# A decoder layer's channel stage on two halves of 528 tokens, seven products for each block

## The chip, the cores and the metric

The kernel runs on one core of a Trainium2 chip. The metric is the device time of one execution in microseconds: 1078.13 us is the median of three runs of the kernel before (1078.03 to 1078.82). TensorE (PE) multiplies matrices into PSUM, which has eight banks of 2 KB per partition; VectorE (DVE), ScalarE (ACT) and GpSimd (POOL) work on SBUF and PSUM, each with its own queue of instructions in a fixed order; SyncE (SP) issues most transfers.

## The reference

One decoder layer on 1056 tokens (1024 of a prompt and 8 x 4 decode tokens), with 1024 channels, 2816 hidden channels (22 chunks of 128) and float32 throughout. What the change touches begins at the norm ahead of the feed-forward part:

```
    m, pool_state = _pool_mixer(u, pool_prev, pos0, w_pool, pool_scale)
    mix = jnp.concatenate([a, m], axis=-1) @ w_out
    x = x + _rms(mix, n_mix_post)
    f = _rms(x, n_ffn_pre)
    f = (jax.nn.silu(f @ w_gate) * (f @ w_up)) @ w_down
    x = x + _rms(f, n_ffn_post)
    x = x + jax.nn.sigmoid(x @ w_ple_gate) * (p @ w_ple)
    return x, k_state, v_state, pool_state
```

## The kernel before

Channels lie on partitions and tokens along the free axis. TensorE reads float32 in a rounded form, so each operand is split into a high and a low part (`split`: a cast on ACT at L167, a subtraction on DVE at L168), and each product is three matmuls, high x high, high x low and low x high (`gemm`, L126 for each matmul). Each matmul loads its own 128 x 128 weights.

The tokens form three groups of 352 (`N`), one matmul wide each. From the channel norm on, groups 0 and 1 are taken together in Strassen's way (Winograd's form): a 2 x 2 block product with seven products in place of eight, named P1, P2, P4, S1 to S4, over operands B11, B21, B22 and T1 to T4, which are sums of the blocks of the input; for the gate and up products the two block columns are the two token groups, the block rows are the gate and up rows of one chunk, and the sum runs over two halves of 512 channels. S1 to S4 also need sums of weights, formed on POOL (L1132). Group 2 is computed directly with eight quarter products. `WALK` sets the order: five slabs of two chunks for group 2 alone, which stand beside the norms of groups 0 and 1, then eleven slabs for the other two or for all. The direct down products of group 2 (`down`) are interleaved with them (`downs`).

The hidden activations of groups 0 and 1 are combined to the seven operands (`pair_put`), split, and written to DRAM (`stage`, `spill`); `down7` reloads them (`x_get`) and works the down product in steps of `STEPS`: a product of a few chunk pairs at a time into one or four banks, which are then added into SBUF (L1286). After it come the norm of the result, the residual, and the last stage: sigmoid of a gate product (seven products again for groups 0 and 1, `ple_first` and `ple_rest`; eight for group 2, `ple_out`) times an embedding product (`embed`).

The order of work is the order in which the code issues it, with norms and similar chains of DVE and ACT work kept as generators (`chain`, `step`, `finish`) that are advanced between matmuls as these are issued (`turn`). Weights are loaded and split some items ahead (`need`, `w_load`). PSUM is a pool of eight single banks. Ahead of twelve products a matmul of 64 columns is issued (`spacer`).

Of the kernel before, what the change touches and what calls it, by code (L numbers as in the profile page):

```python
# [10 lines left out]
F32 = mybir.dt.float32  # L11
# [28 lines left out]
AHEAD = 5  # L40
# [11 lines left out]
W_RAW = 3  # L52

# [8 lines left out]
def trunk_kernel(  # L62
# [38 lines left out]
    psum = ctx.enter_context(tc.tile_pool(name="psum", bufs=8, space=bass.MemoryType.PSUM))  # L101
# [27 lines left out]

    def bank():  # L130
        return psum.tile([P, 512], F32, tag="b", name=nm("b"))

    def tmp(n, s="t", dt=F32):
        return spool.tile([P, n], dt, tag="tmp", bufs=5, name=nm(s), padded_shape=[P, NX])

    def kept(s):
        return spool.tile([P, N], F32, tag="hk", bufs=4, name=nm(s))
# [76 lines left out]
    FIRST2 = tuple(range(NSLAB - 2 * AHEAD, NSLAB, 2))  # L214
    WALK = [(s, (2,)) for s in FIRST2]
    WALK += [(s, (0, 1) if s in FIRST2 else (0, 1, 2)) for s in range(NSLAB)]
    LAST2 = len(WALK) - 1
# [9 lines left out]
    WGU, WD = [], []  # L227

    def down_at(n, i):

        if not n or 2 not in WALK[n - 1][1]:
            return ()
        if 2 in WALK[n][1]:
            return () if i else (0, 1)
        return (i,)

    for n, (s, gs) in enumerate(WALK):
        pairs_of = []
        for i in range(SLAB):
            c = SLAB * s + i  # L240
            jg = direct_item(w_gu[c, 0], [P, KC, P])
            if gs != (0, 1, 2):
                ju = direct_item(w_gu[c, 1], [P, KC, P])
            for j in down_at(n, i):
                WD[n - 1].append(direct_item(w_dn[WALK[n - 1][0], j], [P, SLAB, 512]))
            if gs == (0, 1, 2):
                ju = direct_item(w_gu[c, 1], [P, KC, P])
            js = item("sums", ITEMS[jg][1][0], ITEMS[ju][1][0]) if 0 in gs else None
            pairs_of.append((jg, ju, js))
        WGU.append(pairs_of)  # L250
        WD.append([])
    WD[-1] = [direct_item(w_dn[WALK[-1][0], j], [P, SLAB, 512]) for j in range(2)]
# [3 lines left out]
    QUARTER = {"P1": "11", "P2": "12", "P4": "22"}  # L256
    FIVE, TWO = ("P1", "P4", "P2", "S3", "S2"), ("S1", "S4")
    OPERAND = {"P1": "B11", "P2": "B21", "P4": "T4", "S2": "T2", "S3": "T3", "S1": "T1", "S4": "B22"}
    STEPS = [(k, (0, 1)) for k in FIVE + TWO]
    STEPS += [(k, at) for at in ((2, 3), (4, 5)) for k in FIVE]  # L260
    STEPS += [(k, (2, 3, 4, 5)) for k in TWO]
    SUMS_AT = ["P2", "P2"] + ["P4"] * 4
    WDN = {}
    for k, at in STEPS:
        for e in at:
            WDN[k, e] = item("quarter" if k in QUARTER else "dsum", k, e, at if e == at[-1] else ())
    WPE = [[], []]

    def plan_ple(n, m):
        wp = direct_item(w_ple[m // 4], [P, 2, 512]) if m % 4 == 0 else WPE[n][-1][0]  # L270
        WPE[n].append((wp, direct_item(w_pg[m], [P, KC, P])))

    for m in range(KC):
        plan_ple(0, m)


    PAIRS = ((7, 6), (1, 0), (3, 2), (5, 4))
    W1 = {a: WPE[0][a] if a == KC - 1 else None for a, _ in PAIRS}
    wp1 = WPE[0][-1][0]
    wp0 = None  # L280
    for a in (5, 3, 1):
        if a == 3:
            wp0 = item("home", add_plan(w_ple[0], [P, 2, 512]))
        W1[a] = (wp0 if a < 4 else wp1), direct_item(w_pg[a], [P, KC, P])
    RAW2 = {}
    for a, b in PAIRS:
        if a == KC - 1:
            RAW2[a] = tuple(ITEMS[WPE[0][m][1]][1][0] for m in (a, b))
        else:
            ja = ITEMS[W1[a][1]][1][0] if a == 1 else add_plan(w_pg[a], [P, KC, P])  # L290
            RAW2[a] = ja, add_plan(w_pg[b], [P, KC, P])
    HALF = {KC - 1: WPE[0][KC - 2][1]}
    W2 = {}
    for (a, _), (nxt, _) in zip(PAIRS, PAIRS[1:] + PAIRS[:1]):
        if nxt < KC - 1:
            HALF[nxt] = item("half", RAW2[nxt][1])
        W2[a] = HALF[a], item("sums", *RAW2[a])

    in_a.update(ITEMS[W1[a][1]][1][0] for a in (3, 1))
    in_a.update(j for a in (3, 5) for j in RAW2[a])  # L300
# [3 lines left out]
    quarters = {}  # L304

    def q_load(q, e):

        if (q, e) not in quarters:
            n = len(SETS[e])
            shape = [P, n, 512]  # L310
            if q == "11" and e > 1:
                t = wpool.tile(shape, F32, tag="wr", bufs=W_RAW, name=nm("wq"))
            else:
                t = act_tile(shape, s="wq")
            s0 = SETS[e][0]
            row, col = int(q[1]) - 1, int(q[0]) - 1
            nc.sync.dma_start(t, w_dn[s0 : s0 + n, col, :, row, :].rearrange("s p n -> p s n"))
            quarters[q, e] = t
        return quarters[q, e]

    def q_loads(kind, js):
        for q in {"P1": ("11",), "P4": ("22", "21"), "P2": ("12",)}.get(js[0], ()):
            q_load(q, js[1])
# [17 lines left out]
    def need(k, ahead=LOOK):  # L341

        for i in range(len(made), max(k + 1, min(k + ahead + 1, until[0]))):
# [9 lines left out]
            elif kind == "quarter":  # L353
                made[i] = q_split(q_load(QUARTER[js[0]], js[1]))
                if js[0] == SUMS_AT[js[1]]:
                    for n in ("S1", "S3", "S2"):
                        for e in js[2]:
                            q_sum(n, e)
# [1273 lines left out]
```

## Time and profile before

| | |
|---|---|
| median of the runs | 1078.13 us |
| profiled execution, span | 1076.7 us |
| granted clock of TensorE | 0.997 |
| PE busy | 1065.5 us, 6805 matmuls |
| DVE, ACT, POOL busy | 828.7, 525.7, 285.5 us |
| first gate product to last matmul | 264 to 1071 us |
| moved by DMA | 162.01 MB, 150 GB/s |

The span is measured from the first to the last instruction of one profiled execution. In a row of the trace's groups stand line, engine, operation, output <- inputs and shapes, the number of instructions, then the busy time and the mean of one in ns, then the idle time ahead of them and what ended it. In the chain of waits, time and length are followed by the engine and line, or by what the step waited for.

### The profile page before, as it was taken

The page shows a single profiled execution, that of the slowest core. Times are in us where ns is not written, and L with a number is a line of the kernel's source. Part 1 is how long each engine was busy: PE and PEld are TensorE (multiplying, and loading weights), DVE is VectorE, ACT ScalarE, POOL GpSimd, SP SyncE. Part 2 cuts the span into 40 slices and gives each one's busy share as a digit, 9 for nine tenths or more (in the row PEclk, how much of TensorE's full clock was granted, in tenths as well). Part 3 has the DMA queues.
Part 4 walks back from the last instruction along what each step waited for, and adds up shares of the span by engine and source line. Part 5 has one row for each costly group of instructions (what it writes and reads, how often), then busy time and mean ns, then how long its engine had stood idle before and what let it go on. Part 6 is the DMA issues. An engine that isn't in the chain of part 4 may idle for free.

```text
span 1076.7 us, 17467 instructions
## 1 busy us (share of the span) xinstructions
PE 1065.5 (99%) x6805; PEld 1049.6 (97%) x6805; DVE 828.7 (77%) x1229; ACT 525.7 (49%) x951; POOL 285.5 (27%) x213
## 2 busy tenths in 40 slices
PE   9999999999999999999999999999999999999997
PEld 8999988899999999999999999999999999999997
DVE  6766378977979957767758758659668877999898
ACT  8522277776855524344434434434344832476542
POOL 1045022200000032422324223232309076401170
PEclk9999999999999999999999999999999999999999
DMA  8121311352644312352441533614876955836422
GB/s 299 60 72 40 108 54 37 136 217 90 228 154 134 109 40 81 144 186 71 159 168 59 212 114 107 236 43 160 310 267 230 405 189 181 310 114 216 138 67 74
DMA packets 54162, 162.01 MB, mean 150 GB/s; under 512 B 5796, under 2 KB 20164, under 8 KB 54080
## 3 DMA queue, kind: packets, MB, share of 16 engines
q1 hardware_dynamic: 52752, 159.13, 42.2%
q10 hardware_dynamic: 1328, 1.77, 0.5%
q8 instruction: 53, 0.87, 0.4%
q14 instruction: 29, 0.24, 0.1%
HBM read 123.02 MB, written 37.86 MB: 149 GB/s over the span
## 4 chain that ended last, share of the span: by engine, by line
PE 91%; DVE 5%; ACT 2%; issue 1%; DMA 0%; ACTq 0%; SPq 0%; DVEq 0%
PE b L126 90%; DVE sl L168 1%; DVE sg L1439 1%; PE b L120 1%; DVE u L1286 1%; DVE ql L168 1%; DVE yo L1440 1%; DVE p L1476 0%; DMA xr<-in_x_dram 0%; ACT a L780 0%; DVE w L168 0%; DVE acc L930 0%; ACT qh L167 0%; DVE u L1476 0%; ACT sg L1436 0%
## 5 line engine op out<-in xcount | busy, mean ns | idle before, releaser
L126 PE MATMUL b<-fh,wh 128*128 128x352 f32 x720 | 231.4, 322 | 0.0
L126 PE MATMUL b<-fl,wh 128*128 128x352 f32 x716 | 229.3, 320 | 0.0
L126 PE MATMUL b<-fh,wl 128*128 128x352 f32 x716 | 229.2, 320 | 0.0
L1132 POOL TENSOR_TENSOR wr<-wr 128x512 f32<-128x512 f32 x47 | 69.1, 1470 | 538.1 <-DVE wl L168 512.4
L168 DVE TENSOR_TENSOR wl<-wr,wh 128x1024 fp32r<-128x1024 f32 (+1 forms) x123 | 162.9, 1326 | 51.3 <-ACT wh L167 51.2
L167 ACT CAST wh<-wr 128x1024 fp32r<-128x1024 f32 (+1 forms) x123 | 126.1, 1027 | 123.1 <-PE b L126 96.5
L126 PE MATMUL b<-xo,qh 128*128 128x352 f32 x620 | 147.7, 321 | 0.5 <-ACT u L1314 0.5
L126 PEld LDWEIGHTS b<-fh,wh 128*128 128x128 f32 x720 | 134.9, 188 | 0.0
L126 PE MATMUL b<-fh,sh 128*128 128x352 f32 x420 | 134.6, 322 | 0.0
L126 PEld LDWEIGHTS b<-fl,wh 128*128 128x128 f32 x716 | 134.5, 188 | 0.0
L126 PE MATMUL b<-fh,sl 128*128 128x352 f32 x416 | 133.2, 320 | 0.9 <-DVE sl L168 0.9
L126 PEld LDWEIGHTS b<-fh,wl 128*128 128x128 f32 x716 | 134.1, 187 | 0.0
L126 PE MATMUL b<-fl,sh 128*128 128x352 f32 x416 | 133.2, 320 | 0.0
L126 PE MATMUL b<-h,wh 128*128 128x352 f32 x480 | 112.6, 325 | 1.4 <-ACT h L504 1.2
L126 PEld LDWEIGHTS b<-xo,qh 128*128 128x128 f32 x620 | 107.1, 188 | 0.7 <-ACT u L1314 0.7
L126 PE MATMUL b<-xo,ql 128*128 128x352 f32 x308 | 99.1, 322 | 1.4 <-DVE ql L168 1.2
L339 POOL TENSOR_TENSOR wq<-wq,wq 128x512 f32<-128x512 f32 x44 | 77.4, 1797 | 66.0 <-DVE ql L168 56.3
L167 ACT CAST st<-c 128x352 fp32r<-128x352 f32 x55 | 26.8, 487 | 122.8 <-DVE c L1201 96.6
L126 PEld LDWEIGHTS b<-h,wh 128*128 128x128 f32 x480 | 83.3, 190 | 2.5 <-ACT h L504 1.4
L168 DVE TENSOR_TENSOR sl<-wr,sh 128x1024 fp32r<-128x1024 f32 x47 | 59.5, 1266 | 33.1 <-ACT sh L167 33.1
L126 PE MATMUL b<-hid,wh 128*128 128x352 f32 x352 | 84.0, 321 | 0.0
L126 PEld LDWEIGHTS b<-fh,sl 128*128 128x128 f32 x416 | 77.9, 187 | 1.2 <-DVE sl L168 1.2
(211 smaller groups left out, 2177.8 us busy)
## 6 DMA issues: line engine op xcount, KB each, us to landing
wr<-in_w_gu_dram SPq DMA_DIRECT2D x64, 512.0 KB, 3.4
xd<-st SPq DMA_DIRECT2D x35, 704.0 KB, 4.9
xo<-xd SPq DMA_DIRECT2D x35, 704.0 KB, 6.1
wr<-in_w_dn_dram SPq DMA_DIRECT2D x22, 512.0 KB, 4.2
wq<-in_w_dn_dram SPq DMA_DIRECT2D x20, 512.0 KB, 9.6
wr<-in_w_pg_dram SPq DMA_DIRECT2D x10, 512.0 KB, 3.5
x<-in_x_dram SPq DMA_DIRECT2D x6, 704.0 KB, 9.1
x1d<-x SPq DMA_DIRECT2D x6, 704.0 KB, 3.3
```

Source lines behind the costliest of these rows:

```text
L120: ins = te.transpose(out, src, ident)
L126: ins = te.matmul(*args, **kw)
L167: fix(se.copy(hi, src))
L168: fix(ve.tensor_tensor(lo, src, hi.bitcast(F32), op=ALU.subtract))
L339: ge.tensor_tensor(*(q_load(q, e)[:, i, :] for q in (out, a, b)), op=op)
L1132: ge.tensor_tensor(out, a, b, op=op)
L1286: ve.tensor_tensor(out, a, b, op=ALU.add)
L1439: ve.tensor_tensor(sg[:, v], sg[:, v], pp[:, v], op=ALU.mult)
L1440: ve.tensor_tensor(yo[:, v], sg[:, v], xm[:, v], op=ALU.add)
```

## The change

From the channel norm on, the 1056 tokens form two halves of 528, each in two runs of 264 columns (`QN`, `HN`), and all of them take the seven products; no group is computed directly. A tile of 264 columns has rows 320 apart (`PITCH`). PSUM is a pool of four pairs of banks; a product fills one run per bank, and one DVE or ACT instruction evicts both runs.

- The first product P1 and the gate's C11 = P1 + P2 are made ahead of the blocks, for each run by itself and in the order `AHEAD`, because the tokens become ready group after group; the parts are written to DRAM (`p_d`), and read again in `chunk`. The gate weights are loaded for this once more.
- `chunk` makes the other five products for one block.
- `down` takes one product after the other over all 11 chunk pairs, with its four output tiles in all four PSUM pairs. Operands are written unsplit, reloaded for each product and split then. The weight sums are made on POOL with 1024 columns at a time (`down_form`).
- `ple_steps` and `finished` are the norm and residual of a half; the last stage takes pairs of output tiles, all of them with seven products.
- The spacers are removed.

```diff
-AHEAD = 5
+QN = T // 4
+HN = 2 * QN
+PITCH = 320
+
+
+PARTS = {0: ((1, 0, 0, 352),), 1: ((0, 352, 0, 176), (1, 352, 176, 176)), 2: ((0, 0, 0, 352),)}
+FIRST = 14
...
-    psum = ctx.enter_context(tc.tile_pool(name="psum", bufs=8, space=bass.MemoryType.PSUM))
+    psum = ctx.enter_context(tc.tile_pool(name="psum", bufs=4, space=bass.MemoryType.PSUM))
...
+    def pair():
+        return psum.tile([P, 2, 512], F32, tag="b", name=nm("b"))
+
+    spare = []
+
     def bank():
-        return psum.tile([P, 512], F32, tag="b", name=nm("b"))
+        if spare:
+            return spare.pop()
+        t = pair()
+        spare.append(t[:, 1, :])
+        return t[:, 0, :]
...
+    def row(s="r"):
+        return tmp(HN, s).rearrange("p (i n) -> p i n", n=QN)
+
+    def runs(dt=F32, s="f"):
+        return act_tile([P, 4, PITCH], dt, s)[:, :, :QN]
...
+    AHEAD = [(c, (0,)) for c in range(FIRST)]
+    AHEAD += [(c, (0, 1)) for c in range(FIRST, FFC)]
+    AHEAD += [(c, (1,)) for c in range(FIRST)]
...
+        if k == "S2":
+            keeps[e] = r[0]
+            add(r[0], r[0], r[1], ALU.add)
+            add(r[0], r[0], r[2], ALU.subtract)
+        elif k == "S3":
+            add(r[0], r[0], r[1], ALU.subtract)
+        elif k == "S1":
+            add(r[0], keeps[e], r[0], ALU.add)
+        elif k == "S4":
+            add(r[0], r[0], keeps[e], ALU.subtract)
+        hl = w_tile(r[0].shape, "qh"), w_tile(r[0].shape, "ql")
+        split(*hl, r[0])
...
-    def spacer(w, x):
-        mm(bank()[:, :SPACER], w, x[:, :SPACER], start=True, stop=True)
...
+    def product(w, x, onto=None):
+
+        ps = pair()[:, :, :QN] if onto is None else onto
+        for i in range(2):
+            gemm(ps[:, i, :], ops4(w, x, i), onto=onto is not None)
+        return ps
...
+    def ahead(w, c, i):
+
+        wg = need(w)
+        ps = bank()[:, :QN]
+        gemm(ps, ops4(quarter(wg, 0), operand("B11", i), i))
+        st = row("st")
+        se.copy(st[:, 0, :], ps)
+        if second:
+            second.pop()()
+
+        def rest():
+            gemm(ps, ops4(quarter(wg, 1), operand("B21", i), i), onto=True)
+            se.activation(st[:, 1, :], ps, AF.Silu)
+            nc.sync.dma_start(p_d[c][:, :, i, :], st)
+
+        second.append(rest)
...
+    def seven(w, sums, p1, x, last):
+
+        p4 = product(need(w), x("T4"))
+        s = need(sums)
+        add(p1, p1, product(s["S2"], x("T2")))
+        u4 = row("u4")
+        if not last:
+            add(u4, p1, product(s["S4"], x("B22")))
+        u3 = row("u3")
+        add(u3, p1, product(s["S3"], x("T3")))
+        c21 = row("c21")
         add(c21, u3, p4)
-        ve.tensor_tensor(c21, c21, c11, op=ALU.mult)
-        p5 = product(s["S1"], f7["T1"])
+        yield c21
+        p5 = product(s["S1"], x("T1"))
         add(u3, u3, p5)
-        add(p1, p1, p5)
-        add(p1, p1, product(s["S4"], f7["B22"]))
-        se.activation(p1, p1, AF.Silu)
-        ve.tensor_tensor(u3, u3, p1, op=ALU.mult)
-        if late is None:
-            pair_put(pair, slot, c21, u3)
+        yield u3
+        if last:
+            add(p1, p1, p5)
+            yield p1, product(s["S4"], x("B22"))
         else:
-            late.append((pair, slot, c21, u3))
-
-    os_ = [None] * G
-
-    def down(n, m):
-        wh, wl = need(WD[n][m // 4])
+            add(u4, u4, p5)
+            yield u4
...
+    def chunk(c):
+
+        part_load(c + 2)
+        p = parts.pop(c)
+        p1, c11 = p[:, 0], p[:, 1]
+        made7 = seven(*WG[c], p1, operand, False)
+        c21 = next(made7)
+        add(c21, c21, c11, ALU.mult)
+        c22 = next(made7)
+        c12 = next(made7)
+        se.activation(c12, c12, AF.Silu)
+        add(c22, c22, c12, ALU.mult)
+        chunk_put(c, c21, c22)
...
+    def finished(b):
+
+        for h in range(2):
+            sqs = [runs(s="sq") for _ in range(2)]
+            for sq, o in zip(sqs, os_[b][h]):
+                se.activation(sq, o, AF.Square)
+            add(sqs[0], sqs[0], sqs[1])
+            if h == 0:
+                first = sqs[0]
+                yield 8, 0
+        add(first, first, sqs[0])
+        yield 16, 0
+        acc3[b] = tmp(HN, "acc")
+        add(acc3[b].rearrange("p (i n) -> p i n", n=QN), first[:, 0:2, :], first[:, 2:4, :])
+        for m in range(KC):
+            o = os_[b][m // 4][m % 4 // 2][:, 2 * (m % 2) : 2 * (m % 2) + 2, :]
+            se.activation(o, o, AF.Identity, scale=gn[:, 3, m : m + 1])
+        yield 5, 0
...
+    def x_get(n):
+        if n < len(DOWN) * NSLAB:
+            k, c = DOWN[n // NSLAB], n % NSLAB
+            t = runs(F32R, "xo")
+            src = t[:, 2:4, :].bitcast(F32)
+            nc.sync.dma_start(src, spilled[OPERAND[k], c])
+            split(t[:, 0:2, :], t[:, 2:4, :], src)
+            xops[n] = t
+
+    def down(k, banks, onto=False, ends=None, order_=(0, 1, 2, 3)):
+
+        n0 = DOWN.index(k) * NSLAB
+        for e, ps in enumerate(SETS):
+            for i, c in enumerate(ps):
+                x_get(n0 + c + 3)
+                wh, wl = need(WDN[k, e], 2)
+                t = xops.pop(n0 + c)
+                for j in order_:
+                    cols = slice(j * P, (j + 1) * P)
+                    if banks[j] is None:
+                        banks[j] = pair()[:, :, :QN]
+                    for q in range(2):
+                        gemm(
+                            banks[j][:, q, :],
+                            [(wh[:, i, cols], wl[:, i, cols], t[:, q, :], t[:, 2 + q, :])],
+                            c == 0,
+                            c == NSLAB - 1,
+                            onto=onto,
+                        )
+                    if c == NSLAB - 1:
+                        ends(j, banks[j])
...
+    for w, (c, qs) in zip(WA, AHEAD):
+        for i in qs:
+            ahead(w, c, i)
+    second.pop()()
+    part_load(0)
+    part_load(1)
+    for c in range(FFC):
+        chunk(c)
+        if c == FFC - 1:
+            for n in range(3):
+                x_get(n)
+
+    share[0] = 0.5
+    u = out_half()
+    banks = [None] * 4
+    down("P1", banks, ends=lambda j, ps: se.copy(at_j(u, j), ps))
+    os_[0][0] = c11 = out_half()
+    down("P2", banks, onto=True, ends=lambda j, ps: se.copy(at_j(c11, j), ps))
+    down("S2", [None] * 4, ends=lambda j, ps: add(at_j(u, j), at_j(u, j), ps))
+    u3 = out_half()
+    down("S3", [None] * 4, ends=lambda j, ps: add(at_j(u3, j), at_j(u, j), ps))
+    os_[0][1] = c21 = out_half()
+    down("P4", [None] * 4, ends=lambda j, ps: add(at_j(c21, j), at_j(u3, j), ps))
+    chain(ple_steps(0, 1e6), 8)
+    n = len(summed)
+
+    def both(j, ps):
+        v = row("p5")
+        se.copy(v, ps)
+        add(at_j(u, j), at_j(u, j), v)
+        add(at_j(u3, j), at_j(u3, j), v)
+
+    down("S1", [None] * 4, ends=both)
+    while len(summed) == n:
+        step(chains[0])
+    step(chains[0])
+    down("S4", [None] * 4, ends=lambda j, ps: add(at_j(u, j), at_j(u, j), ps))
+    os_[1] = [u, u3]
...
+    finish(list(chains))
     share[0] = 0.7
...
+    chain(ple_steps(1, 12), 4)
+    p1s = {}
+    for a, _ in PAIRS:
+        w = need(W1[a])
+        ps = product(quarter(w, 0), e7["B11"])
+        p1s[a] = row("p1")
+        se.copy(p1s[a], ps)
+        xm = x2_row(a, 0)
+        pp = embed(WE[a // 4], a, 0)
+        product(quarter(w, 1), e7["B21"], ps)
+        ple_end(ps, xm, pp, a, 0)
+    for w, h in ((WE[0], 0), (WE1, 1)):
+        for a, b in PAIRS:
+            if a // 4 == h:
+                for m, half_ in ((b, 0), (b, 1), (a, 1)):
+                    embed_early(w, m, half_)
     for a, b in PAIRS:
...
+        last = (a, b) == PAIRS[-1]
+        xm = {x: x2_row(*x) for x in ((b, 0), (b, 1), (a, 1))}
+        made7 = seven(*W2[a], p1s[a], gate_operand, last)
+        for x in ((b, 0), (b, 1), (a, 1)):
+            v = next(made7)
```

On TensorE, inside the gate and up loop, at a border of two products (the names are the PSUM tile, the high or low part of the operand, and the high or low part of the summed weights). Before:

```order
L126 MATMUL b_6171<-fl_3647,sh_6058 128x352
L126 MATMUL b_6171<-fh_3646,sl_6059 128x352
L126 MATMUL b_6186<-fh_3847,sh_6054 128x352
L126 MATMUL b_6186<-fl_3848,sh_6054 128x352
L126 MATMUL b_6186<-fh_3847,sl_6055 128x352
```

And now:

```order
L133 MATMUL b_6699<-fh_4358,sh_6302 128x264
L133 MATMUL b_6699<-fh_4356,sl_6303 128x264
L133 MATMUL b_6728<-fh_4417,sh_6302 128x264
L133 MATMUL b_6728<-fh_4419,sh_6302 128x264
L133 MATMUL b_6728<-fh_4417,sl_6303 128x264
```

The three matmuls per product and their weights are the same; each has 264 columns, and a product runs through its weights twice, once for each run.

On ACT, where the down stage goes from S1 to S4 (L1339 copies S1's four results out of PSUM; `acc` is the sum of squares, and L427 makes its inverse root from the pair `b_10496`):

```order
L1339 COPY p_10462<-b_10097 128x528
L189 CAST xo_10506<-xo_10506 128x2x264
L1339 COPY p_10472<-b_10104 128x528
L1339 COPY p_10482<-b_10118 128x528
L189 CAST xo_10553<-xo_10553 128x2x264
L1339 COPY p_10492<-b_10125 128x528
L427 ACT_TABLE_LOAD
L427 ACTIVATE acc_10254<-b_10496,c_86 128x528
```

Before, the mean had a bank of its own out of eight; now its pair is one of four, and its reader stands behind the four copies.

On ACT, at the head of the last stage. Before (L1423 copies an embedding out of PSUM, L1436 is the sigmoid, L1254 scales the down result):

```order
L167 CAST wh_9993<-wr_9952 128x1024
L1254 ACTIVATE u_8425<-u_8425,c_72 128x352
L1436 ACT_TABLE_LOAD
L1436 ACTIVATE sg_10047<-b_10005 128x352
L167 CAST wh_9999<-wr_9991 128x1024
L1423 COPY pp_10053<-b_10054 128x352
```

And now (L1402 copies a first part P1 out of PSUM, L1386 is the sigmoid, L1216 squares, L1227 scales):

```order
L1402 COPY p_10941<-b_10904 128x528
L189 CAST wh_10892<-wr_10884 128x1024
L1386 ACT_TABLE_LOAD
L1386 ACTIVATE sg_10988<-b_10904 128x528
L189 CAST wh_10898<-wr_10890 128x1024
L189 CAST pl_10911<-pr_10913 128x4x264
L1216 ACTIVATE sq_10936<-o_8278 128x4x264
L1216 ACTIVATE sq_10937<-o_8279 128x4x264
L1216 ACTIVATE sq_10964<-o_9368 128x4x264
L1216 ACTIVATE sq_10965<-o_9369 128x4x264
L1227 ACTIVATE o_8278<-o_8278,c_72 128x2x264 x2
L1227 ACTIVATE o_8279<-o_8279,c_72 128x2x264 x2
```

Two more such rows of L1227 (o_9368, o_9369) follow, and behind them stands the next copy, of `b_10999`, onto which TensorE goes on adding. Before, the scaling at the border was the last of several that stood among the down products, one tile of 352 columns at a time; now squares and scalings of a whole half stand as one block in the last stage.

More of the change, by code (lines that the diff above doesn't have):

```diff
@@ L321, in q_loads @@
[L321 to L339 removed]
+    keeps = {}
@@ new lines, in plans, with down_form, add @@
+    def plans(kind, js):
+        return DN_LOADS[js] if kind == "down" else js
+    def down_form(k, e):
+        r = [raws[j] for j in DN_LOADS[k, e]]
+        def add(out, a, b, op):
+            ge.tensor_tensor(out, a, b, op=op)
+        if k == "S2":
+            keeps[e] = r[0]
[9 more added lines that the diff above has]
+        split(*hl, r[0])
+        return hl
@@ L381, in trunk_kernel, with step @@
     share = [0.6]
+    def step(ch):
+        try:
+            load, wait = next(ch[0])
+        except StopIteration:
+            chains.remove(ch)
+            return
+        dve[0] = max(dve[0], now[0]) + load / share[0]
+        ch[1] = dve[0] + wait
     def turn(n):
@@ new lines, in ffn_steps @@
+            yield 18, 0
+        if g:
+            i = 2 - g
+            for h in range(2):
+                key = f"B{h + 1}1"
+                if i == 0:
+                    fx[key] = [[runs(F32R, "fh") for _ in range(2)] for _ in range(2)]
+                for t in range(2):
+                    split(*(by_chunk(x[t])[:, :, i, :] for x in (*fx[key], raw[0][h])))
+                    yield 5, 0
+                ready.add((key, i))
+            return
+        yield from sum_steps(fx, *raw)
@@ new lines, in sum_steps, with sums, keep @@
+    def sum_steps(to, first, second):
+        (b11, b21), (b12, b22) = first, second
+        def sums(out, a, b):
+            for t in range(2):
+                ve.tensor_tensor(out[t], a[t], b[t], op=ALU.subtract)
+        def keep(key, src):
+            to[key] = [[runs(F32R, "fh") for _ in range(2)] for _ in range(2)]
+            for t in range(2):
+                split(to[key][0][t], to[key][1][t], src[t])
+        sums(b11, b12, b11)
+        yield 16, 0
+        sums(b12, b22, b12)
+        yield 16, 0
+        keep("B22", b22)
+        yield 16, 0
+        sums(b22, b22, b11)
+        yield 16, 0
+        sums(b21, b21, b22)
+        yield 16, 0
+        for key, src in (("T4", b21), ("T2", b22), ("T3", b12), ("T1", b11)):
+            keep(key, src)
+            yield 16, 0
@@ L1082, in stage @@
[L1082 to L1097 removed]
+    share[0] = 0.6
@@ new lines, in trunk_kernel, with embed_early, x2_row, ple_end @@
+    held = []
+    def embed_early(w, m, b):
+        if not held:
+            t = runs(s="pp")
+            held[:] = t[:, 0:2, :], t[:, 2:4, :]
+        early[m, b] = held.pop()
+        se.copy(early[m, b], embed(w, m, b))
+    def x2_row(m, b):
+        t = row("xm")
+        nc.sync.dma_start(t, x2d[b][m // 4][:, m % 4, :].rearrange("p (i n) -> p i n", n=QN))
+        return t
+    def ple_end(gate, xm, pp, m, b, parts=1, into=None):
+        sg = row("sg")
+        n = QN // parts
+        for i in range(0, QN, n):
```

743 lines of the change are left out of this document (202 added, 541 removed).

## The prediction

> **What bounds the kernel now.** I read the page first: busy time by engine, then the chain that ended last.
>
> ```profile
> span 1076.7 us, 17467 instructions
> PE 1065.5 (99%) x6805; PEld 1049.6 (97%) x6805; DVE 828.7 (77%) x1229; ACT 525.7 (49%) x951; POOL 285.5 (27%) x213
> PE 91%; DVE 5%; ACT 2%; issue 1%; DMA 0%; ACTq 0%; SPq 0%; DVEq 0%
> core 0: 1076.7 us, clock 0.997
> ```
>
> TensorE is busy 99% of the span and carries 91% of the chain, at full clock (0.997). The time is the number of matmuls times the interval between two of them, and a little waiting. The profiled execution has a span of 1076.7 us; the measured median, 1078.13, is 1.4 us above it, which I add at the end. Second, the chain row by row, and the span in stretches that I chose at the stages' borders:
>
> ```profile
> 208.20 618.03 PE b L126 x3894
> 827.65 81.00 PE b L126 x508
> 926.65 0.86 DVE u L1286 x2
> 928.70 92.78 PE b L126 x581
> ...
> 264.00:372.00 108.00, 108.00 (x682) 108.00 (x681) 99.44 (x124) 66.82 (x88) 0.00 (x0) 1.00 0.48 159
> 372.00:826.00 454.00, 454.00 (x2859) 454.00 (x2859) 324.67 (x485) 182.83 (x281) 140.43 (x99) 1.00 0.42 147
> 826.00:967.00 141.00, 139.15 (x871) 138.21 (x870) 116.83 (x129) 73.70 (x118) 60.88 (x34) 1.00 0.70 252
> 967.00:1071.00 104.00, 103.02 (x649) 102.44 (x647) 96.91 (x113) 53.11 (x81) 28.13 (x16) 1.00 0.37 125
> 1071.00:1076.70 5.70, 0.00 (x0) 0.00 (x0) 2.81 (x9) 0.70 (x2) 0.00 (x0) 0.68 0.27 95
> ```
>
> (Behind each stretch: its length, then busy time and count of PE, weight loads, DVE, ACT, POOL, then clock, DMA share, GB/s.) The first row is 618.03 us without a single wait, 618.03/3894 = 158.7 ns per matmul. The gate and up products begin here:
>
> ```profile
> 263.77 0.32 PE L126 MATMUL b<-mh,wl 128*128 128x352 f32 x1
> 263.93 0.32 PE L126 MATMUL b<-fh,wh 128*128 128x352 f32 x1
> ```
>
> From 264 to 1071 us TensorE works on what the change rewrites, 807 us; ahead of it nothing changes, behind it 5.7 us of tail remain. The code gives 5028 products of 352 columns there: 5028 x 0.159 = 799.5 us, so waits and small matmuls make up only about 8 us.
>
> **The change, part by part.**
>
> *Matmuls.* Gate and up go from 22 x 132 = 2904 matmuls to 22 x 168 = 3696, down from 1452 to 7 x 264 = 1848, the gate of the last stage from 528 to 672, the embedding from 144 to 192: 5028 become 6408, each of 264 columns in place of 352. Columns fall from 1,769,856 to 1,691,712, by 4.4%; matmuls rise by 27%. All depends on the interval t of a 264-column matmul that brings its own weights, and before has none. These rows bound it, with the cold clock at the start of the program and a place where one of 64 columns (a spacer) stands between two others:
>
> ```profile
> 8.63 1.38 PE L126 MATMUL b<-h,wl 128*128 128x352 f32 x4
> 9.80 1.08 PE L126 MATMUL b<-h,wh 128*128 128x352 f32 x3
> ...
> 8.60:9.80 1.20, 1.20 (x6) 1.20 (x5) 1.20 (x3) 0.48 (x1) 0.00 (x0) 0.50 1.06 400
> ...
> 371.99 0.32 PE L126 MATMUL b<-fh,wl 128*128 128x352 f32 x1
> 372.00 0.35 PEld L126 LDWEIGHTS b<-fh,wh 128*128 128x128 f32 x2
> 372.15 0.43 PE L126 MATMUL b<-fh,wh 128*128 128x64 f32 x2
> 372.26 0.19 PEld L126 LDWEIGHTS b<-fl,wh 128*128 128x128 f32 x1
> 372.43 0.32 PE L126 MATMUL b<-fl,wh 128*128 128x352 f32 x1
> ```
>
> Four matmuls at a granted clock of 0.50 take 9.80 - 8.63 = 1.17 us, 293 ns each: 1.2 columns per ns. At full clock that would be 2.4, and 352 columns 147 ns; measured are 159, so about 12.3 ns per matmul come on top of the columns. **Fixed surcharge:** 264/2.4 + 12.3 = 122.3 ns. **Wholly proportional:** 159 x 264/352 = 119.3 ns. **Below:** the two loads in the row at 372.00 end together at 372.35, and one takes 0.19, so the second starts at 372.16, with the short matmul; the next load starts at 372.26, about 110 ns later, though TensorE has nothing else to do by then. A matmul with weights of its own cannot be shorter, so t is at least some 112 ns. **Above:** if columns were handled in whole pieces of 64, 352 would be 6 pieces, 384/2.4 = 160 ns, near the 159 measured, and 264 would be 5 pieces, 133.3 ns; the cold 293 ns (352/1.2, not 384/1.2 = 320) speak against it. I take the fixed surcharge, because each matmul keeps one whole weight load beside it: 6408 x 0.1223 = 783.7 us, 16 us under the 799.5 of before.
>
> The Trainium skill, "TensorE: Matmul & The Clock Gate", section "Back-to-back issue gap", gives N/2.4 + 2.5 ns when warm. For 352 columns that is 149 ns, and this trace has 159, so the measurement decides; by the page's formula 264 columns would be 112.5 ns and the stream 721 us. The same page, section "LDWEIGHTS (loading the stationary operand)", gives P/1.2, 107 ns for 128 columns, with which the 110 ns above agree.
>
> *Waits that the change adds.* Durations for 528 and 1056 elements are drawn on straight lines through these rows:
>
> ```profile
> L1229 DVE TENSOR_TENSOR o<-o,b 128x352 f32<-128x352 f32 x80 | 37.4, 512 | 1.1 <-PE b L126 1.0
> L1104 DVE TENSOR_TENSOR u<-u,u 128x352 f32<-128x352 f32 x11 | 6.8, 618 | 0.0
> L1364 DVE TENSOR_TENSOR u<-u,acc 128x1408 f32<-128x1408 f32 x4 | 6.5, 1620 | 0.1
> L168 DVE TENSOR_TENSOR sl<-wr,sh 128x1024 fp32r<-128x1024 f32 x47 | 59.5, 1266 | 33.1 <-ACT sh L167 33.1
> L1423 ACT COPY pp<-b 128x352 f32<-128x352 f32 x16 | 6.8, 457 | 3.6 <-PE b L126 3.5
> L1254 ACT ACTIVATE u<-u,c 128x352 f32<-128x352 f32 x16 | 8.7, 580 | 0.1
> L1241 ACT ACTIVATE sq<-o 128x1408 f32<-128x1408 f32 x2 | 2.6, 1374 | 0.0
> L167 ACT CAST wh<-wr 128x1024 fp32r<-128x1024 f32 x95 | 99.6, 1048 | 78.2 <-PE b L126 52.4 <-issue 24.8 <-ACT sl L1177 0.9
> L1436 ACT ACT_TABLE_LOAD x2 | 2.6, 1283 | 0.0
> L1132 POOL TENSOR_TENSOR wr<-wr 128x512 f32<-128x512 f32 x47 | 69.1, 1470 | 538.1 <-DVE wl L168 512.4
> L339 POOL TENSOR_TENSOR wq<-wq,wq 128x512 f32<-128x512 f32 x44 | 77.4, 1797 | 66.0 <-DVE ql L168 56.3 <-PE b L126 9.7
> wq<-in_w_dn_dram SPq DMA_DIRECT2D x20, 512.0 KB, 9.6
> ```
>
> DVE: 0.69 us for 528 from PSUM, 1.28 for 1056. ACT: 0.61 for a copy of 528, 0.73 scaled, 1.08 for 1056.
>
> - *Blocks.* One block is 120 matmuls, 14.7 us. DVE has eight 528-column operations (5.5 us), splits (3.4) and two sums (1.5): 10.4 us, 71%; before, 324.67 of 454 is 72%. Weights are still split a block ahead, so this is hidden: 1 us (0 to 3). If DVE were late, each block would pay. The new weight loads (80 for 64 of 512 KB) and the partial products written and read back lie beside it at a DMA share of 0.42: nothing.
> - *The products made ahead* share their time with the norm of the two other groups and table loads on ACT, 44 pieces of 24 matmuls: 3 us (0 to 6).
> - *Down, product by product.* A product holds all eight PSUM banks, so its four evictions stand between it and the next; the first is covered by the three pairs still running (18 matmuls, 2.2 us), a split ahead of it on the queue (1.27) uses that up now and then. Six changes at 0.5: 3 us (0 to 6). The sums for S2 are two POOL operations on 1024 columns for each set of two block pairs: twice 1470 or 1797 each, so 5.9 to 7.2 us, against 48 matmuls, 5.9 us; the operands are reloaded at the same time, with 9.6 us to landing already now. Six sets: 5 us (0 to 15).
> - *S1 to S4.* The pair of banks for the mean of squares is read by ACT only behind S1's four copies and a table load (1.28), and by DVE behind eight additions; S4's fourth pair waits for it: 3 us (1 to 5).
> - *Head of the last stage.* The second gate product cannot add onto its PSUM pair until ACT has copied the first part out, and on ACT's queue the copy stands behind a table load (1.28), a sigmoid (0.62), two casts (1.05, 1.08), four squares (4.3), eight scalings (5.8): with itself 14.7 us. Its cover is 24 + 12 matmuls, 4.4 us: **10 us** (6 to 13) of waiting. The same for the third: 2 us. Then T4's operand: after the norm DVE owes sixteen additions and subtractions and four splits of 1056 (25.6), six operations on 528 (4.5) and five splits of weights (5), 35 us, and TensorE gets there about 6 us (2 to 9) early. In before's chain waits of this kind are short (0.86 us at 926.65).
>
> Waits: 1 + 3 + 3 + 5 + 3 + 10 + 2 + 6 = 33 us, of which the separate bounds make 15 to 45 likely. The 8 us of small matmuls and waits of before go with the old code; some 2 us of small matmuls (mean of squares) stay.
>
> **Sum.** 264 + 783.7 + 2 + 33 + 5.7 = 1088.4 us of span, and 1.4: **1090 us**. With waits of 15 to 45: 1072 to 1102.
>
> **Rivals.**
> - *Proportional interval* (119.3 ns): 764.5 us of stream, 1071 us; with the bounds of the waits 1053 to 1083. For it: 159 ns at one size alone cannot tell a share from a constant. Against: cold matmuls show no share at all. This is the mechanism on the other side: it decides as soon as t is under some 120 ns, where the sum with 33 us of waits meets 1078.
> - *The surcharge nearly vanishes, the weight load is the floor* (112 to 116 ns): 1024 to 1050 us. The page's formula is here. Against it: the trace shows 12 ns where it has 2.5.
> - *Whole pieces of 64 columns* (133.3 ns): 854 us of stream, 1160 us, 8% slower. For it: 159 ns is within 1 ns of six pieces; against it, the cold rows.
> - *The waits don't come* (under 15 us), because queues run further ahead than I count; with 122.3 ns: 1060 to 1072 us.
> - That the change doesn't do what it says is small here: the order of the program shows 6408 matmuls of 264 columns.
>
> **How the numbers follow.** Forecast (fixed surcharge, 15 to 45 us) 0.50: nearly all of it slower. Proportional 0.17, mostly faster; floor 0.12, faster; pieces 0.11, slower; no waits 0.10, faster. Within 0.2% is about what a measurement of this kernel can tell from no change. Faster: 0.05 + 0.13 + 0.12 + 0.09 = 0.39. Same: 0.05 + 0.01 + 0.01 = 0.07. Slower: 0.40 + 0.03 + 0.11 = 0.54. The likeliest case alone spans 1072 to 1102. The range leaves out the pieces and the lower half of the floor, about 0.2 in all: 1042 to 1112.
>
> **What would show it.** In the profile of the changed kernel: the interval in the block loop (122 or 119, 113, 133 ns); the chain's rows at the head of the last stage, with ACT's squares and scalings in them, 10 us, and T4's operand behind DVE; at the changes of the down products, waits for DVE and ACT, and for POOL in S2; DVE near 71% in the block loop with no waits. An interval under 120 ns, or waits of less than 15 us, would make the forecast wrong in sign.

## The result

The changed kernel takes 1271.59 us (median of four runs, 1269.39 to 1276.55) against 1078.47 us of the kernel before: 1.179 times as long, with a 95% interval of 1.177 to 1.182. The profiled execution has a span of 1274.8 us. The forecast was slower, but by 1%, not by 18%. The head of its page:

```profile
span 1274.8 us, 20358 instructions
PE 1105.5 (87%) x8175; PEld 1065.5 (84%) x8175; DVE 778.4 (61%) x1058; ACT 492.7 (39%) x871; POOL 281.7 (22%) x199
PE 66%; DVE 10%; ACT 9%; issue 6%; DMA 4%; POOL 3%; SPq 1%; DVEq 0%; ACTq 0%; POOLq 0%
```

TensorE is now busy 87% of the span and has 66% of the chain, where it had 99% and 91%; no other engine has become busier. So it is waiting. The span in stretches tells where; they are cut at the first gate product, the first S product, the first down product, the first product of the last stage and the last matmul:

```profile
0.00:382.80 382.80, 297.06 (x1754) 267.91 (x1754) 195.51 (x388) 156.41 (x391) 52.79 (x65) 0.92 0.22 77
382.80:556.90 174.10, 146.41 (x1087) 139.34 (x1088) 99.90 (x114) 97.67 (x161) 11.05 (x8) 0.95 0.61 198
556.90:874.30 317.40, 317.40 (x2619) 317.40 (x2618) 215.79 (x290) 76.63 (x100) 110.64 (x81) 1.00 0.54 182
874.30:1131.30 257.00, 232.75 (x1854) 230.83 (x1853) 164.72 (x157) 102.48 (x141) 75.26 (x30) 0.95 0.62 203
1131.30:1268.40 137.10, 111.81 (x870) 110.01 (x868) 99.75 (x106) 58.82 (x77) 31.98 (x16) 0.90 0.40 134
```

The forecast had a span of 1088.4 us; this one is 186 longer. By stretch, measured against what the forecast's own terms give for it:

| stretch | forecast | measured | |
|---|---|---|---|
| up to the first gate product | 263.9 | 382.8 | +118.9 |
| products made ahead, and the first P4 (1080 matmuls) | 135.1 | 174.1 | +39.0 |
| blocks (2616 matmuls) | 320.9 | 317.4 | -3.5 |
| down | 237.0 | 257.0 | +20.0 |
| last stage | 123.7 | 137.1 | +13.4 |

The largest part lies in the stage of which the prediction says "ahead of it nothing changes". The matmuls there are the same. In the trace of before the stage reads:

```profile
0.00:264.00 264.00, 261.29 (x1752) 246.96 (x1753) 187.99 (x374) 148.52 (x384) 56.02 (x65) 0.99 0.32 110
```

TensorE stood still for 2.7 us of it and does so for 85.7 now (382.80 - 297.06). The other 36 us are the same matmuls at a lower granted clock, 0.92 in place of 0.99: 297.06 us of busy time in place of 261.29. The largest waits of TensorE from 130 to 300 us, by what it waited for (total, times, longest), and one wait earlier on in the order of time:

```profile
PE b L133 <- DVE ml L675: 7.2, 4, 2.3
PE b L133 <- DVE a L812: 6.8, 3, 2.8
PE b L133 <- DVE a L794: 6.3, 5, 1.3
...
78.90 0.49 PE L133 MATMUL b<-h,wh 128*128 128x352 f32 x2
...
79.58 0.53 DVE L688 TENSOR_TENSOR a<-b,acc 128x352 f32<-128x352 f32 x1 [2.59 <-PE b L133]
...
80.25 0.56 PE L133 MATMUL b<-h,wh 128*128 128x352 f32 x2 [0.71 <-DVE a L688]
```

DVE evicts the product that TensorE has just finished, and TensorE waits for precisely that eviction before it begins the next product, in another bank. In the order of the program two such products carry one name:

```
L133 MATMUL b_548<-h_333,wh_138 128x352 [waits DVE_49]
...
L133 MATMUL b_548<-h_333,wh_142 128x352 [waits DVE_49]
```

Both are banks of the tile `b_548`. `DVE_49` counts the instructions that DVE has finished. In the program the first product waits for the 56th, which empties the tile that held these two banks before (`b_325`), and the second for the 67th, which is the last to read the first half of `b_548` itself. The changed `bank()` takes a pair of banks as one tile and hands out its halves to two products that have nothing to do with each other. That gives the theory for the experiments: **dependencies follow the tile, so the product in the second bank waits until the first has been evicted.** In `chunk`, where one product fills both banks, this costs nothing (no wait in 317 us); in the first stage, whose code the change leaves alone, and in the products made ahead (20 waits for ACT's copy of P1, 19.7 us) the product in the second half of a tile waits.

### The profile page after: what moved, and what is told of

Its sections match the earlier page's. It is cut to its first block, busy times and chain, and to the rows that moved or that the text cites. A ratio compares the mean times of both kernels' runs of the same rounds, so it can differ in the third digit from the quotient of the medians.

```text
span 1274.8 us, 20358 instructions
## 1 busy us (share of the span) xinstructions
PE 1105.5 (87%) x8175; PEld 1065.5 (84%) x8175; DVE 778.4 (61%) x1058; ACT 492.7 (39%) x871; POOL 281.7 (22%) x199
## 4 chain that ended last, share of the span: by engine, by line
PE 66%; DVE 10%; ACT 9%; issue 6%; DMA 4%; POOL 3%; SPq 1%; DVEq 0%; ACTq 0%; POOLq 0%
PE b L133 66%; POOL wr L1112 2%; DMA xo<-xd 2%; ACT wh L189 1%; DVE wl L190 1%; POOL a L306 1%; ACT a L754 1%; DMA wr<-in_w_dn_dram 1%; ACT o L1227 1%; DMA pr<-in_p_dram 1%; DVE o L1136 1%; DMA xr<-in_x_dram 1%; DVE a L794 1%; ACT sq L1216 1%; DVE xo L190 1%
## 5 line engine op out<-in xcount | busy, mean ns | idle before, releaser
L133 PE MATMUL b<-fh,sh 128*128 128x264 f32 x1664 | 304.0, 284 | 0.0
L133 PEld LDWEIGHTS b<-fh,sh 128*128 128x128 f32 x1664 | 258.1, 189 | 0.0
L133 PE MATMUL b<-xo,qh 128*128 128x264 f32 x1232 | 231.2, 289 | 24.3 <-DVE o L1136 8.1
L133 PE MATMUL b<-fh,sl 128*128 128x264 f32 x832 | 235.7, 283 | 0.0
L133 PEld LDWEIGHTS b<-xo,qh 128*128 128x128 f32 x1232 | 195.7, 193 | 26.2 <-issue 9.6
L133 PE MATMUL b<-xo,ql 128*128 128x264 f32 x616 | 177.1, 288 | 0.0
L133 PE MATMUL b<-fh,wh 128*128 128x264 f32 x704 | 138.3, 296 | 29.5 <-ACT st L1150 19.7
L133 PEld LDWEIGHTS b<-xo,ql 128*128 128x128 f32 x616 | 119.0, 193 | 0.0
L133 PEld LDWEIGHTS b<-h,wh 128*128 128x128 f32 x480 | 90.7, 207 | 24.6 <-DVE ml L675 6.7
L133 PE MATMUL b<-fh,wl 128*128 128x264 f32 x352 | 101.8, 289 | 0.0
L133 PE MATMUL b<-fh,w 128*128 128x264 f32 x624 | 83.8, 290 | 9.4 <-ACT fh L189 6.7
```

Source lines behind the costliest of these rows:

```text
L133: ins = te.matmul(*args, **kw)
```

## The experiments

### The shared tile, from four sides

e1 gives every bank its own tile until the products made ahead are done, and opens the pool of pairs then:

```diff
-    psum = ctx.enter_context(tc.tile_pool(name="psum", bufs=4, space=bass.MemoryType.PSUM))
+    singles = ExitStack()
+    one = singles.enter_context(tc.tile_pool(name="one", bufs=8, space=bass.MemoryType.PSUM))
+    psum = [None]
...
     def bank():
+        if psum[0] is None:
+            return one.tile([P, 512], F32, tag="b", name=nm("b"))
...
     second.pop()()
+    singles.close()
+    psum[0] = ctx.enter_context(tc.tile_pool(name="psum", bufs=4, space=bass.MemoryType.PSUM))
```

> The changed kernel, but until the last of the products made ahead each bank of PSUM is a tile of its own (eight of them), and the pool of four pairs opens only behind that. Theory (two banks in one tile: a matmul into the second bank waits until the first has been evicted): the first gate product moves from 382 back to 264 us (within 3), the products made ahead take 130 to 140 us in place of 174, and the blocks and all behind them stay as they are, so the span falls from 1275 to 1110-1125 us. Rival (the start is slow for another reason, such as the larger row buffers or the transfers): the first gate product stays at 360 to 385 us and the span above 1240.

e2 does the reverse in the kernel before: pairs handed out in halves up to the first gate product, single banks behind it.

> The kernel before, with only this edit: until the gate and up products begin, its banks are taken two by two out of four tiles of two banks. Theory: the first gate product moves from 264 to 375-390 us, with waits of about 0.95 us where a matmul goes into the second bank of a tile, and the span becomes 1190 to 1205. Rival (something else of the change slows the start): it stays at 264-275 and the span under 1095.

e3 is the kernel before with `bufs=6` in place of 8.

> The kernel before with six single banks in place of eight. Rival to the shared tile (depth: a tile of two banks is freed as late as its later half, which leaves six to seven banks in turn): the first gate product would come at 350 us or later. Theory: single banks are freed one by one and six do nearly as well as eight in the first part, so the first gate product comes at 264 to 280 us. The down products, with four banks at a time, may lose some us in both.

e4 is e1 with the pool changed ahead of the loop over `AHEAD`.

> As e1, but the pool of pairs opens ahead of the products made ahead, so only these use two banks of one tile. Theory: the first gate product at 264 us as in e1, the products made ahead take 170 to 178 us as in the changed kernel, span 35 to 45 us above e1 (about 1155). Rival (this phase is bound by DVE and ACT work of the norms, not by the banks): it takes the same time as in e1, within 6 us.

e2, e3 and e4 were run once each, e1 and all later kernels four times. Of e1, e2 and e3 the row in which the gate products begin (e2 has the wait ahead of it in brackets), then the stretches of e1 and of e4:

```profile
264.55 0.40 PE L135 MATMUL b<-fh,wh 128*128 128x264 f32 x2
```

```profile
383.46 0.43 PE L128 MATMUL b<-fh,wh 128*128 128x352 f32 x1 [1.79 <-ACT sq L939]
```

```profile
270.17 0.32 PE L126 MATMUL b<-fh,wh 128*128 128x352 f32 x1
```

```profile
0.00:264.60 264.60, 261.59 (x1754) 247.37 (x1755) 189.12 (x385) 148.24 (x388) 54.73 (x65) 0.99 0.31 110
264.60:408.40 143.80, 135.07 (x1088) 133.65 (x1087) 100.87 (x117) 97.90 (x165) 10.35 (x8) 0.98 0.75 243
408.40:725.80 317.40, 317.40 (x2618) 317.40 (x2618) 214.50 (x288) 76.46 (x100) 111.41 (x81) 1.00 0.55 181
```

```profile
267.20:437.50 170.30, 147.59 (x1086) 139.99 (x1087) 100.76 (x115) 97.71 (x162) 9.44 (x7) 0.95 0.61 197
437.50:751.50 314.00, 314.00 (x2619) 314.00 (x2618) 215.06 (x289) 76.45 (x100) 111.90 (x82) 1.00 0.56 186
```

With single banks the gate products begin at 264.6 us as before, and the clock of the first stage is back at 0.99 (e1); the kernel before, with halves of pairs and nothing else changed, begins them at 383.5 (e2), and its span goes from 1076.7 to 1199.5. Depth is not the cause: six single banks cost 6 us there, not 119 (e3). The products made ahead take 143.8 us with single banks and 170.3 with halves (e4), so 26.5 us of that stretch are the same cause; e1's 143.8 is above the 130 to 140 that were expected. e1 as a whole takes 1124.93 us (1.041 times before, 1.038 to 1.044): the shared tile is worth 147 of the 193 us that the change costs, and what is left is 46 us. Of e4 the span is only 24 us above e1, where 35 to 45 were expected: its gate products begin 2.6 us later, but its blocks run 3.4 us shorter (taken up below) and its last stage 1.2.

### The waits behind it

All further runs build on e1. In its down and last stage TensorE stands still for 22 and 25 us (254.70 - 232.47 and 137.00 - 111.84):

```profile
725.80:980.50 254.70, 232.47 (x1854) 230.54 (x1853) 163.79 (x159) 102.43 (x141) 76.17 (x30) 0.96 0.63 206
980.50:1117.50 137.00, 111.84 (x870) 110.02 (x868) 99.69 (x106) 58.71 (x77) 31.96 (x16) 0.90 0.40 134
```

e5 reloads the operands of the down stage six chunk pairs ahead and splits them two ahead, in place of three and three; e6 makes P1 of two gate tiles ahead of the norm of the second half.

```diff
-                x_get(n0 + c + 3)
+                x_load(n0 + c + 6)
+                x_get(n0 + c + 2)
```

```diff
-    chain(ple_steps(1, 12), 4)
...
+    open_gate(7)
+    open_gate(5)
+    chain(ple_steps(1, 12), 0)
```

> e1 (1123.8 us of span in its profile), and in the down stage the operands are reloaded six chunk pairs ahead and split two ahead, in place of both three ahead. Theory (at a change of product the evictions stand on DVE behind splits of operands whose reloads are late): the wait of 7.2 us where S2 goes over to S3 falls under 2, that of 3.0 us at the first chunk pair of the stage under 1, and at S1 to S4 some 2 to 3 of 7.1 us go; the span falls by 8 to 12 us. Rival (DVE and POOL are simply behind by then, whatever the reloads do): the waits stay and the span moves by less than 3 us.

> e1, and at the head of the last stage the first parts P1 of two gate tiles are made and copied ahead of the norm's block of squares and scalings on ACT. Theory A (the wait of 14.3 us for a copy behind that block is a loss of its own): it falls to under 5 us and the span by 9 to 12. Theory B (the block is the first half of one chain through ACT and DVE to the operand T4, and whoever waits less for its first half waits more for its second): the wait of 14.3 goes, those ahead of T4 (13 us in all) grow by nearly as much, and the span falls by 0 to 4 us.

e8 has both.

> e5 and e6 together. If the down stage's waits (theory of e5) and the head of the last stage (theory B) are independent, the span is e1 less the gains of both, 8 to 16 us below e1, about 1110; still above the 1077 of before, since the waits left in the products made ahead (about 10 us), in S2 (5 us) and ahead of T4 (over 10 us) are not touched.

Waits of TensorE in the last stage, of e1 and then of e6:

```profile
PE b L135 <- ACT p L1408: 14.0, 1, 14.0
PE b L135 <- ACT fh L193: 6.7, 2, 4.9
PE b L135 <- DVE fh L194: 2.6, 2, 1.9
PE b L135 <- ACT sg L1392: 1.7, 1, 1.7
```

```profile
PE b L135 <- ACT fh L193: 13.8, 2, 13.0
PE b L135 <- ACT sg L1392: 5.2, 2, 3.0
PE b L135 <- ACT hl L412: 3.4, 1, 3.4
PE b L135 <- DVE fh L194: 2.2, 2, 1.5
```

In e6 the copy of P1 is waited for no more, but 14.0 + 6.7 + 2.6 + 1.7 = 25.0 us became 13.8 + 5.2 + 3.4 + 2.2 = 24.6. The median is 1125.45 us, e1's 1124.93, and the last stage takes 139.1 us in e6's profile for 137.0 in e1's. That is theory B: squares, scalings, root, residual and the sums up to T4 are one chain through ACT and DVE behind the last down product, and TensorE has too little other work for its length. Moving one wait only shows the next, though not all of it at T4 as theory B has it: the waits for T4's operand (`fh`) grow from 9.3 to 16.0 us, and the rest comes at the sigmoid (`sg`) and at the mean of squares (`hl`). The last wait for T4 ends 77 us after the stage's beginning in e1 and 79 us in e6.

e5 gained little (1122.54 us): the wait from S2 to S3 went from 7.2 to 5.7 us from start to start, and the one in the stage's first chunk pair stayed at 3.0. From S1 to S4 it went from 7.1 to 6.0, but one of 3.0 for ACT's copies of S1 came beside it. The down stage takes 255.9 us for e1's 254.7, and of the 4 us in the span 3.5 are the blocks, which run at 120.0 ns there (below). That is nearer to its rival. e8 came out at 1124.57 us, with no gain over e5, against its expectation. (e1, e4, e6 and e11, whose edits lie outside of the down stage, take 253.0 to 257.0 us in it, so a difference of a few us there says little.)

e10 takes the reloads from SP's queue to ACT's. e9 moves S1's eight additions in the code behind two steps of the norm, e12 has e9 and e10 together, and e13 is e10 with the additions held behind the norm's reader on DVE.

```diff
-            nc.sync.dma_start(t[:, 2:4, :].bitcast(F32), spilled[OPERAND[k], c])
+            nc.scalar.dma_start(t[:, 2:4, :].bitcast(F32), spilled[OPERAND[k], c])
```

```diff
     step(chains[0])
+    ordered[0] = True
+    step(chains[0])
+    ordered[0] = False
+    for j, v in p5s:
+        for t in (u, u3):
+            tc.keep_in_program_order(ve.tensor_tensor(at_j(t, j), at_j(t, j), v, op=ALU.add))
```

> e5, and at the change from S1 to S4 the eight additions of S1's result are issued behind the two steps of the norm that read the mean's pair of banks, in place of ahead of them. Theory (the pair of the mean is freed late because its reader on DVE stands behind eight additions, 4.95 us): the wait at S4's fourth pair falls from 6.0 to 1-2 us, the span by 3 to 5 us. Rival (it is ACT's table load and root, or the matmuls of the mean, that come late): the wait stays over 4 us.

> e5, with the reloads of the down stage's operands issued by ACT's DMA queue in place of SP's. Theory (on SP's queue a reload stands behind loads of weights that wait for one of three raw buffers, which POOL's sums hold): the operands come earlier, the wait of 5.7 us where S2 goes over to S3 falls under 2 us and that of 3.0 us at the second operand of the stage goes; the span falls by 4 to 8 us. Rival (the transfers themselves are the limit, 237 GB/s over these 42 us at a share of 0.74, or POOL): the waits stay within 2 us of e5.

> e9 and e10 together: the best form of the changed kernel that these runs point to. Span 8 to 12 us under e5's 1119.7, so 1108 to 1112; slower than before's 1077 by some 3%, as the waits in the products made ahead (12 us), in S2 (5) and at the head of the last stage (27) stay.

> e10 with S1's eight additions held behind the step of the norm that reads the mean's pair on DVE; in e9 and e12 the additions were moved in the code, but stood ahead of that reader on DVE's queue all the same, as in e5 and e10. Theory (the reader behind eight additions, 4.95 us): the wait at S4's fourth pair, 4.9 us in e10, falls to 1 us or less; the span falls by 3 to 5 us unless the operand splits behind it take it back. Rival (ACT's four copies, table load and root come last): it stays at 4 us or more.

e14 leaves out the second of POOL's two operations for S2's weights.

> e10 with the second of POOL's two operations for each set of S2's weights left out, so that S2 multiplies by another sum of weights; the transfers are all there. Theory P (POOL's 5.9 us a set, 11.45 us for two, hold the raw buffers and with them the loads): the wait of 11.3 us where S2 goes over to S3 falls under 6 us, and S2 to S3 take 4 to 8 us less. Theory D (the loads of 512 KB, 4.4 to 7.4 us each there against 3.8 in the median, are the limit): it stays at 9 us or more.

Waits of TensorE in the down stage, of e5, e10, e13 and e14:

```profile
PE b L135 <- DVE o L1140: 6.0, 2, 5.4
PE b L135 <- DVE sq L435: 5.5, 1, 5.5
PE b L135 <- ACT o L1344: 5.0, 2, 4.3
```

```profile
PE b L135 <- DVE o L1140: 11.7, 2, 11.0
PE b L135 <- DVE sq L435: 4.6, 1, 4.6
PE b L135 <- DVE u L1140: 0.9, 1, 0.9
```

```profile
PE b L135 <- DVE o L1140: 13.1, 2, 12.5
PE b L135 <- DVE u L1140: 2.0, 1, 2.0
PE b L135 <- DVE sq L435: 1.8, 1, 1.8
```

```profile
PE b L135 <- DVE o L1139: 11.7, 2, 11.0
PE b L135 <- DVE sq L434: 7.9, 1, 7.9
PE b L135 <- DVE u L1139: 0.9, 1, 0.9
```

*S1 to S4* (the row of `sq`, which reads the mean's pair). In e9 the additions stand ahead of that reader on DVE's queue in spite of their place in the code, and the wait stays at 5.0 us; e9 (1126.63 us) says nothing on the theory, and e12 nothing either (1117.94 us and a span of 1115.4, where 1108 to 1112 were expected). e13 puts them behind it, and the wait goes from 4.6 to 1.8 us; in the other runs, where the additions come first, it is 4.6 to 8.4. So the additions were most of it, if not down to the 1 us expected; the price in the forecast (3 us) was too low. The time is hardly any shorter for it: the down stage takes 246.9 us in e13 for 246.4 in e10, as the wait from S2 to S3 is 1.5 us longer and that for `u` 1.1. The span goes from 1116.2 to 1111.5 us, but 3.5 us of that are the blocks, at 121.3 ns in e10 and 120.0 in e13.

*S2 to S3* (the row of `o`). With the reloads on ACT's queue the waits where P2 goes over to S2 go (the row of ACT `o`, which copies P2's results; 5.0 to 0.7), but the one at the end of S2 doubles, where the theory had it fall under 2 us; the down stage takes 246.4 us in place of 255.9, and the median falls to 1115.47. So the gain is there, the wait named for it is not. e14 (1114.36 us) halves POOL's work for S2's weights, and the wait does not move from 11.0 us. So it isn't POOL's time; the chain of waits of e14 in that stretch names the loads of weights:

```profile
802.79 5.79 DMA wr<-in_w_dn_dram
...
808.60 4.79 DMA wr<-in_w_dn_dram
...
813.54 2.76 POOL wr L310
816.31 4.18 DMA wr<-in_w_dn_dram
```

For the sums of S2 three of the four blocks of weights are loaded, and operands beside them. e10's stretch from 792 to 837 us has a DMA share of 0.77 at 251 GB/s. That the transfers as such are the limit, rather than the three raw buffers and the order in which they come free, isn't shown: SBUF has no room for a further raw buffer beside the rest, and no run separates the two. It stays open.

### The interval of a matmul

e7 puts the rows of 264 columns directly behind each other; e11 puts one matmul of 64 columns behind the first block.

```diff
-PITCH = 320
+PITCH = 264
```

```diff
         chunk(c)
+        if c == 0:
+            w, x0 = need(WG[1][0]), operand("T4")
+            mm(pair()[:, 0, :64], w[0][:, 0, :], x0[0][0][:, 0, :64], start=True, stop=True)
```

> e1 with rows of 264 columns directly behind one another (PITCH 264 in place of 320). The interval of the 264-column matmuls in the blocks is 121.3 ns with rows 1280 bytes apart. Theory (a fixed surcharge beside each matmul, whatever the address): 120 to 122 ns, span within 4 us of e1. Rival (rows that do not begin at a multiple of 256 bytes cost another piece): 125 ns or more in the blocks, span 15 us or more above e1.

> e1 with one matmul of 64 columns behind the first block. In e1 the blocks run at 121.3 ns for each matmul (a repeating 120, 121, 126, 124, 116), in e5 at 120.0. Theory (the stream of matmuls runs in one of several rhythms that it keeps until something breaks it, and a short matmul breaks it): 121.3 ns ahead of the short matmul and 120.0 behind it, the blocks 3 us shorter. Rival (the rhythm comes from the addresses of this kernel's tiles): 121.3 ns on both sides.

The same 310 us of the block loop in e1, e5 and e7 (behind the length: busy time and count of PE), and the blocks of e11 behind its short matmul:

```profile
410.00:720.00 310.00, 310.00 (x2557) 310.00 (x2557) 210.98 (x283) 72.16 (x94) 110.65 (x80) 1.00 0.54 179
```

```profile
410.00:720.00 310.00, 310.00 (x2586) 310.00 (x2585) 214.40 (x287) 75.63 (x99) 110.15 (x80) 1.00 0.55 185
```

```profile
410.00:720.00 310.00, 310.00 (x2550) 310.00 (x2549) 210.87 (x283) 72.92 (x94) 111.84 (x81) 1.00 0.55 182
```

```profile
419.20:719.00 299.80, 299.80 (x2501) 299.80 (x2500) 206.82 (x278) 72.36 (x94) 106.44 (x78) 1.00 0.55 181
```

310/2557 = 121.2 ns in e1, 310/2586 = 119.9 in e5, 310/2550 = 121.6 in e7 and 299.8/2501 = 119.9 in e11. The address of the rows matters little (e7). In e11 the intervals from start to start read 120, 121, 126, 124, 116 and again from the beginning up to the short matmul, and 122, 117, 121 behind it: the stream keeps a rhythm until something breaks it, and at the short matmul it went from 121.3 to 120.0. In no other profile does the interval change inside the blocks: it is 121.3 from end to end in the changed kernel, e1, e9 and e10, and 120.0 in e4, e5, e6, e8, e12, e13 and e14, without a short matmul and with the same code for the blocks. The blocks of e11 are 3 us shorter than those of e1. Its median isn't (1123.78 us, 1118.31 to 1125.66, against 1118.55 to 1125.65 of e1); e11's profile is of its fastest run and e1's of its slowest. Both vary by 7 us between runs, and what differs between these, or how often a short matmul changes the rhythm, isn't shown.

## Why the prediction failed

- **"Ahead of it nothing changes" is the step that failed,** and with it the price of 3 us for the products made ahead. The prediction took the change's extent from the place where its new code begins, and weighed the pool of pairs only where new code uses it (evictions in down, the mean's pair). But `bank()` serves the stage ahead as well. The rows of matmuls stand there unchanged in the order of the program; what changed is what they wait for. e1, e2 and e4 show 118 to 119 us in the first stage and 26 in the products made ahead. No rival had this mechanism, and the range ended at 1112 us.
- **A second term was put at nothing: the clock behind a wait.** The sum counts each matmul at full clock, as before had it in all of these stages. In e1 the granted clock is 0.98, 0.96 and 0.90 in the three stages with waits. 132 matmuls there start 180 to 235 ns after the one ahead of them in place of 121, which is 13 us in all: 2.6 in the products made ahead, 6.3 in down, 4.2 in the last stage. Behind the wait from S1 to S4 (TensorE goes on at 948.6 us), 20 matmuls take 4.42 us, 221 ns each; in the next 7 us the clock is full again:

```profile
946.20:953.00 6.80, 4.42 (x20) 4.42 (x21) 6.80 (x9) 0.00 (x0) 2.77 (x1) 0.50 0.01 2
953.00:960.00 7.00, 7.00 (x59) 7.00 (x59) 6.90 (x7) 2.03 (x2) 0.00 (x0) 1.00 0.80 259
```

- *The interval of a 264-column matmul*: forecast 122.3 ns, measured 121.3 in the changed kernel and 119.9 to 121.6 in all runs, between the fixed surcharge and proportion (119.3). The runs at 121.3 lie nearer to the one, those at 120.0 nearer to the other, so the two aren't told apart by them. On 6408 matmuls, 122.3 to 121.3 is 6 us to the good. The floor of the weight load (112 to 116) and the pieces of 64 columns (133.3) fall. The Trainium skill, "TensorE: Matmul & The Clock Gate", section "Back-to-back issue gap", gives N/2.4 + 2.5 ns, 112.5 here, for a single matmul by itself, and says of a stream of weight loads and matmuls that both set the spacing; the prediction put the formula to the stream. The trace is above it by 7 to 9 ns here, as it was by 10 at 352 columns, and the measurement decides.
- *Blocks:* forecast 1 us of waits, measured none; DVE busy 215.79 of 317.40 us, 68% for the 71% forecast.
- *Products made ahead, without the shared tile* (e1): 143.8 us for 135.1. The cause was named (copies on ACT beside the norms; 7.2 of the 8.7 us of waits there are for them), the size was 9 us short.
- *Down:* 254.7 us in e1 for 237.0, with 22.2 us of waits for the 11 forecast. The 5 us for POOL's sums in S2 hold: 4.7 are waited for ACT's copies where P2 goes over to S2, and in e1's chain the last of these stands behind a cast that waits for POOL. S1 to S4 was named with its mechanism, and priced at 3 where 7 were measured in e1. The change from S2 to S3 was put under "six changes at 0.5"; it is 7 us by itself, because in e1's chain DVE's evictions stand behind splits of operands that come late. Late reloads were weighed for S2 alone.
- *Head of the last stage:* 18 us were forecast (10 + 2 + 6), about 25 measured. The copy behind ACT's squares and scalings is there (14.0 us for 10, above the bound of 13). But the sum treated it and T4 as separate losses; e6 shows one chain, whose total doesn't change when the first wait is removed.
- The sum with single banks would have been 1088 us of span; e1 measures 1123.8, so even without the failed step the forecast was 35 us short, and e1's 1124.93 us lies above the range too. TensorE stands still for 8.7 + 22.2 + 25.2 = 56 us in e1's three stages, where the forecast had 33 and at most 45, and the matmuls behind the waits are slow. The sign would have held: the proportional rival's condition, an interval under 120 ns, was met in some runs, but the waits left no room for it. The best form that was run, e13, takes 1111.36 us, 1.029 times before (1.027 to 1.031). No version here beats the kernel before.

## What to carry to other kernels

When a helper that hands out buffers changes, go through all of its callers, those outside of the rewritten stage first, and compare what their instructions wait for, not only their order. Two independent results in one tile are tied together: share a tile between banks only where one product fills it and one instruction empties it. And where two waits belong to one chain of dependent work, price the chain against the work that covers it, not each wait by itself. Look at the granted clock behind each long wait, and price the slower matmuls there with it.

## What was unexpected of the hardware

A stream of equal matmuls has more than one steady rhythm: 264 columns at 120.0 or at 121.3 ns, in every interval (e5) or in repeating patterns of three or five (116 to 126 ns), in the same code at the same granted clock of 1.00. Inside the blocks the rhythm stayed the same in each profile but one, where it changed at a single matmul of 64 columns (e11). On the 2616 matmuls of the blocks that is 3 us. From 352 to 264 columns the interval fell by 158.7 - 121.3 = 37.4 ns, or 38.7 at 120.0, where 88 columns at 2.4 per ns (the rate that the prediction works out from the rows at a clock of 0.50) are 36.7: most of the part above the columns (12 ns at 352) is still there at 264 (10 to 11 ns).
